# Seven block products instead of eight in two of the four feed-forward halves

## The chip, the cores and the metric

One core of a Trainium2 chip runs the whole kernel. The metric is the time of one execution in microseconds (us) on the device; three runs of the kernel before are given. A profiled execution of its own gives the trace. Engines are named as in the profile: PE is TensorE (matrix products), DVE is VectorE, ACT is ScalarE, POOL is GpSimd, SP is SyncE, which here only issues transfers.

## The reference

Two layers run over 512 tokens of width 1024 (256 context tokens and 256 latent tokens, two streams with their own modulation vectors). Each layer is: a feed-forward half step, a token mixing, and a second feed-forward half step.

```
x = x + 0.5 * mx[2] * _swiglu(_modulate(_rmsnorm(x, g_n1[l]), mx[0], mx[1]), w_ff1_up[l], w_ff1_dn[l])
...
def _swiglu(h, w_up, w_dn):
    a, b = jnp.split(h @ w_up, 2, axis=-1)
    return (jax.nn.silu(a) * b) @ w_dn
```

`w_up` is 1024 x 5632 (gate part a and up part b of 2816 columns each), `w_dn` is 2816 x 1024, all float32. The nine modulation rows `mx[0..8]` of a layer come from `silu(c) @ w_ada[l]`. After the last layer only the latent stream is needed.

## The kernel before

Activations lie with the channels on the 128 partitions and the tokens in the columns: context tokens are columns 0 to 255 (`CTX`), latent tokens 256 to 511 (`LAT`). The hidden width 2816 is 22 blocks of 128 (`FB`). The four halves are called (layer, half): (0,0), (0,1), (1,0), (1,1); the last one handles the latent stream alone. Halves (0,1) and (1,0) follow each other directly, between the two mixings.

**Float32 by parts.** An operand is split into a float32r part (hi) and the rest (lo). A product is three matmuls: hi by hi, hi by lo, lo by hi. Activations after a norm lie in `hh` and `hl`; the gated hidden blocks lie in pairs of their own.

**Weights.** A weight comes in units of 128 x 1024 float32 (512 KB) by the SP queue into a buffer `st` (3 of them). ACT makes `wh` from it (line 224) and DVE makes `wl = st - wh` (line 226). There are `WB` = 5 pairs `wh`, `wl`. A unit is issued up to `AHEAD` = 150 places ahead of the work that uses it, where buffers allow.

**A feed-forward half** (`ff`): the 22 hidden blocks go in two chunks of 11. For each block `i`, the up product gives `pa` (gate) and `pb` (up) in PSUM, 2 x 8 x 3 matmuls of 512 columns; then tanh, three DVE operations and one ACT copy make the gated block and its two parts. After 11 blocks the down product runs: 8 output blocks of 33 matmuls, each added to the residual `x` (line 481). In the second chunk the last two output blocks go by streams, the latent stream first, so that the norm of a stream (`Norm`, `rstd_of`, `newton`, `norm_apply`) runs beside the other's products; the `flush` in the next half's first block does the context norm.

**Modulation.** `Ada` computes modulation columns on DVE: each block of 128 columns is two transfers of 256 KB by the POOL queue and two or four multiply-and-accumulate operations of 128 x 512 (line 375). The blocks are dripped into half (0,0) (56 blocks) and half (0,1) (all 72 of layer 1).

The order of the instructions on each engine is fixed when the program is built, by a scheduler that follows program order and the places ahead; an engine runs its row strictly in that order. Two queues of transfers matter, SP's and POOL's.

Of the kernel before, what the change touches and what calls it, by code (L numbers as in the profile page):

```python
# [8 lines left out]
F32 = mybir.dt.float32  # L9
# [7 lines left out]
P = 128  # L17
# [25 lines left out]
WB = 5  # L43
# [37 lines left out]
def _unit_index():  # L81
    idx, n = {}, 0
    for l in range(DEPTH):
        for ff in range(2):
            if ff == 1:
# [18 lines left out]
                for nb in range(KB):  # L104
                    idx[("out", l, nb)] = n
                    n += 1
            for c in range(2):
# [16 lines left out]
def body(ctx, tc, A):  # L124
# [6 lines left out]
    ap_ = ctx.enter_context(tc.tile_pool(name="ap", bufs=56))  # L131
# [22 lines left out]
    def put_aside():  # L154
        """The residual leaves its room to the token mixing, which needs it only at its end."""
        for j in range(KB):
            nc.sync.dma_start(aside[:, j, :], xs[j])
# [53 lines left out]
    def load(dst, src):  # L211
        """On the SP queue, and at the start behind what the first norm needs."""
# [3 lines left out]
    def unit(key, n, kb):  # L216
        with tc.high_priority(offset=ahead[0]):
            st = wp.tile([P, UW], F32, tag="st", name="st")
# [11 lines left out]
    def units(keys, n, kb):  # L230
        """A weight cut along its rows: a list of (hi, lo) [P, N] blocks."""
# [7 lines left out]
    def mm3(ps, lhs, rhs, lsl=slice(None), rsl=slice(None), late=False):  # L239
        """late: the second parts of rhs come last, as they are not there yet."""  # L240
# [39 lines left out]
    # The engine holds one set of functions at a time: Tanh is in one, Ln in another,  # L280
    # Exp in both.
# [12 lines left out]
    def tanh_half(out, src):  # L294
        """2 sigmoid(x) - 1"""
# [3 lines left out]
    def silu2(out, src):  # L299
        """2 x sigmoid(x)"""  # L300
# [10 lines left out]
    def silu_rows():  # L311
        """Twice the silu of the two conditioning vectors on every partition, in halves."""
# [79 lines left out]
    class Ada:  # L392
        """Modulation blocks, fed into other work; loads run some blocks ahead."""
# [10 lines left out]
        def run(self, frac):  # L404
            """Until this share of the blocks is done."""
# [15 lines left out]
    def newton(r, ss, n, width, t=None):  # L421
        """One step that takes r = rsqrt(ss / width + EPS) to float32's accuracy."""
# [5 lines left out]
    def rstd_of(sq_sum, n, width):  # L428
        """sq_sum: to be summed over the partitions, and over its list."""
# [10 lines left out]
    class Norm:  # L440
        """Sum of squares over the blocks of one stream, added as they come."""
# [26 lines left out]

    def hpairs(cols):
# [4 lines left out]
    def flush():  # L474
        """The norm that a stream still lacks."""
# [99 lines left out]
    def mix(l, after):  # L575
# [12 lines left out]
        class Feed:  # L588
            """Work that stands between the steps of the attentions, whose steps wait
            for each other: products that need no other result soon (step), and the  # L590
            elementwise chains behind them, an operation at a time (pump)."""
# [28 lines left out]
            def advance(self, i):  # L620
                """One step of this item; whether it had one left."""
# [12 lines left out]
            def step(self, n=1, open_=lambda key: True):  # L634
                """n steps of the first items that there is room for."""
# [19 lines left out]
        # two blocks of the queries' width: a bank each, or one for both  # L655
# [13 lines left out]
        def split_gen(jobs, scale=None):  # L669
            """jobs: (source, hi, lo)."""  # L670
# [10 lines left out]
        def conv_start(ps):  # L681
            """The tokens of two segments, each between zeros."""
# [100 lines left out]
            # minus the stabiliser, exactly, and its parts for the product that spreads it  # L783
# [17 lines left out]
        def gate_cols():  # L801
            """As columns of tokens."""
# [17 lines left out]
        def log_sigm(f, e):  # L820
            """f becomes log sigmoid(f)."""
# [9 lines left out]
        # latent projections of the attention  # L831
# [22 lines left out]
        def rope_gen(z, c0, then):  # L854
            """In place on the latent columns of z, which start at c0; then the parts."""
# [13 lines left out]
        def head_parts(z, dst):  # L869
            """By head: both parts of the queries one over the other, as the rows of one product."""  # L870
# [565 lines left out]
```

## Time and profile before

| | |
|---|---|
| three runs | 2394.9, 2396.31, 2396.78 us (median 2396.31) |
| profiled execution, from its first to its last instruction | 2395.4 us |
| PE busy | 98% of the span |
| DVE, ACT, POOL busy | 67%, 41%, 7% |
| half (0,1) | 1030 to 1402 us: first chunk to 1159, its down product to 1220, second chunk to 1343, its down product to 1402 |
| half (1,0) | 1402 to 1775 us: first chunk to 1534, its down product to 1595 |
| mixings | 410 to 1030 us and 1775 to 2190 us |

The span is the profiled execution's whole time, and the medians of the runs are of other executions of the same program; they differ by 0.9 us. A stretch's limit is read from the stretch: an engine that is busy 67% over the whole may be full in one part of it.

### The profile page before, as it was taken

Reading aid. Unit: us, or ns where it says so; the run is one execution under the profiler, and the core shown is the slowest. Engines: PE = TensorE matmul, PEld = TensorE weight load, DVE = VectorE, ACT = ScalarE, POOL = GpSimd, SP = SyncE. Lnnn points to the kernel's source line nnn. Section 1 sums busy time; section 2 is a strip of 40 time slices with the busy share of each in tenths; the row PEclk is TensorE's granted clock in tenths of the full one; section 3 lists DMA queues with packets and bytes.
Section 4 is the critical chain, followed back from the end, with each engine's and each line's share of the span. In section 5 each row is a group of like instructions: output and inputs, shape, how many; then the busy total and the mean of one; then the engine's idle time right before and its main releaser. Section 6 shows DMA issues by size and latency. Waiting matters only on the chain.

```text
span 2395.4 us, 34542 instructions
## 1 busy us (share of the span) xinstructions
PE 2352.9 (98%) x13170; PEld 2008.8 (84%) x13170; DVE 1601.3 (67%) x3375; ACT 990.7 (41%) x1630; POOL 171.9 (7%) x384
## 2 busy tenths in 40 slices
PE   8999999999999999999999999999999999999998
PEld 4888888888888888888888898888887799999998
DVE  7887777786477654479986663334357867776665
ACT  6322223556555442242222242222245654555443
POOL 1112110000010000012231000000000000000000
PEclk9999999999999999999999999999999999999999
DMA  8656444211122222355585322232232223354563
GB/s 317 204 168 228 150 146 158 86 56 53 62 80 71 72 79 97 132 194 186 202 299 187 115 101 99 78 116 89 76 103 80 99 80 106 103 170 152 175 209 117
DMA packets 101251, 316.93 MB, mean 132 GB/s; under 512 B 13150, under 2 KB 15454, under 8 KB 101086
## 3 DMA queue, kind: packets, MB, share of 16 engines
q1 hardware_dynamic: 80606, 247.61, 30.3%
q0 software_dynamic: 20480, 67.13, 8.1%
q8 instruction: 103, 1.69, 0.3%
q14 instruction: 62, 0.51, 0.1%
HBM read 311.54 MB, written 3.15 MB: 131 GB/s over the span
## 4 chain that ended last, share of the span: by engine, by line
PE 95%; DVE 3%; ACT 2%; issue 1%; DMA 0%; DVEq 0%; SPq 0%; ACTq 0%
PE dn L246 20%; PE pa L270 5%; PE pb L270 5%; PE pb L272 5%; PE pa L272 5%; PE pa L271 5%; PE pb L271 5%; PE p L270 4%; PE p L271 4%; PE p L272 4%; PE sc L1159 2%; PE pv L246 2%; PE pa L246 2%; PE pb L246 2%; PE k L270 1%; PE k L271 1%
## 5 line engine op out<-in xcount | busy, mean ns | idle before, releaser
L224 ACT ACTIVATE wh<-st 128x1024 fp32r<-128x1024 f32 (+1 forms) x484 | 471.3, 976 | 945.3 <-PE pb L271 253.6
L226 DVE TENSOR_TENSOR wl<-st,wh 128x1024 fp32r<-128x1024 f32 (+1 forms) x484 | 540.4, 1119 | 374.2 <-ACT wh L224 370.3
L246 PE MATMUL dn<-hi,wl 128*128 128x512 f32 (+1 forms) x674 | 247.7, 367 | 0.0
L246 PE MATMUL dn<-hi,wh 128*128 128x512 f32 (+1 forms) x674 | 247.3, 368 | 0.0
L246 PE MATMUL dn<-lo,wh 128*128 128x512 f32 (+1 forms) x674 | 246.5, 366 | 0.0
L270 PE MATMUL pa<-hh,wh 128*128 128x512 f32 (+1 forms) x640 | 234.4, 366 | 0.0
L270 PE MATMUL pb<-hh,wh 128*128 128x512 f32 (+1 forms) x640 | 234.4, 366 | 0.0
L272 PE MATMUL pa<-hh,wl 128*128 128x512 f32 (+1 forms) x640 | 234.2, 366 | 0.0
L272 PE MATMUL pb<-hh,wl 128*128 128x512 f32 (+1 forms) x640 | 234.2, 366 | 0.0
L271 PE MATMUL pa<-hl,wh 128*128 128x512 f32 (+1 forms) x640 | 234.2, 366 | 0.0
L271 PE MATMUL pb<-hl,wh 128*128 128x512 f32 (+1 forms) x640 | 234.2, 366 | 0.0
L364 POOL DMA_DIRECT2D ada<-ada x256 | 137.2, 537 | 736.0 <-PE dn L246 216.1
L271 PE MATMUL p<-hl,wh 128*128 128x256 f32 (+1 forms) x536 | 179.6, 335 | 0.0
L270 PE MATMUL p<-hh,wh 128*128 128x512 f32 (+1 forms) x512 | 174.1, 340 | 0.0
L272 PE MATMUL p<-hh,wl 128*128 128x512 f32 (+1 forms) x512 | 172.6, 337 | 0.0
L375 DVE SCALAR_TENSOR_TENSOR ada<-ada,cs 128x512 f32<-128x512 f32 x256 | 166.3, 684 | 0.0
L246 PEld LDWEIGHTS dn<-hi,wh 128*128 128x128 f32 x674 | 126.7, 188 | 23.4
L246 PEld LDWEIGHTS dn<-hi,wl 128*128 128x128 f32 x674 | 126.6, 188 | 22.7
L246 PEld LDWEIGHTS dn<-lo,wh 128*128 128x128 f32 x674 | 126.7, 188 | 22.4
L270 PEld LDWEIGHTS pb<-hh,wh 128*128 128x128 f32 x640 | 120.2, 188 | 22.0
L272 PEld LDWEIGHTS pb<-hh,wl 128*128 128x128 f32 x640 | 120.0, 188 | 22.1
L272 PEld LDWEIGHTS pa<-hh,wl 128*128 128x128 f32 x640 | 120.0, 188 | 22.1
(361 smaller groups left out, 4979.1 us busy)
## 6 DMA issues: line engine op xcount, KB each, us to landing
st<-wall SPq DMA_DIRECT2D x340, 512.0 KB, 3.3
ada<-ada POOLq DMA_DIRECT2D x256, 256.0 KB, 3.4
st<-wall SPq DMA_DIRECT2D x72, 384.0 KB, 2.9
st<-wall SPq DMA_DIRECT2D x64, 320.0 KB, 2.9
ada<-ada SPq DMA_DIRECT2D x32, 256.0 KB, 5.4
x<-xT SPq DMA_DIRECT2D x8, 256.0 KB, 5.8
cb<-cc SPq DMA_DIRECT2D x8, 256.0 KB, 5.8
aside<-x SPq DMA_DIRECT2D x8, 256.0 KB, 2.0
```

The costliest lines, as they stand in the source:

```text
L224: S.activation(hi[:, :n], st[:, :n], AF.Copy)
L226: V.tensor_tensor(lo[:, :n], st[:, :n], hi[:, :n].bitcast(F32), ALU.subtract)
L246: TE.matmul(ps, lhs[k][a][:, lsl], rhs[k][b][:, rsl], start=i == 0, stop=i == 3 * n - 1)
L270: TE.matmul(ps, a, b, start=first, stop=False)
L271: TE.matmul(ps, a, bl, start=False, stop=False)
L272: TE.matmul(ps, al, b, start=False, stop=final_)
L364: nc.gpsimd.dma_start(st, ada[ADA[l, g] + j, :, q * 512 : (q + 1) * 512])
L375: V.scalar_tensor_tensor(o, st, 0.5, cb[s, q], ALU.mult, ALU.mult, accum_out=dst)
L1159: TE.matmul(ps[qb], a[:, c], b[:, :nk], start=i == 0, stop=i == len(steps) - 1)
```

## The change

In halves (0,1) and (1,0) the up product of two hidden blocks (a "step"; 11 steps) is written as a product of 2 x 2 blocks. The weight's blocks are a11, a12, a21, a22: the first digit is the part (1 gate, 2 up), the second the half of the 1024 rows. The activation's blocks are the latent and context tokens of each half of the rows. Eight block products become seven: products 1, 2, 3 and 4 have one factor that is a plain block, and 5, 6, 7 work on sums (weights a21+a22, that plus a11, a11+a21; a12 is added for product 3). A block product is 24 matmuls of 256 columns (2 blocks, 4 row blocks, 3 parts). The results are combined where PSUM is read.

- Sums of weights: a21+a22 and the sum with a11 by GpSimd, in place in `st` (L591 of the changed kernel); a11+a21 and the sum with a12 by accumulating transfers of the POOL queue (L589).
- Sums of activations: `seven_lat` and `seven_ctx` take the place of `norm_apply` before these halves; they make the activation sums and their two parts.
- Each of the seven weights of a step is split into two parts (before: four units for the same two blocks).
- Three chunks of 8, 8 and 6 hidden blocks, so three down products (24, 24 and 18 matmuls for each output block) instead of two of 33. Steps run two at a time, interleaved product by product.
- Buffers: `WB` 5 to 4, `st` 3 to 6, activation tiles 56 to 54.
- `Ada`: 24 blocks of layer 1 in half (0,1), the other 48 in half (1,0); before, 72 and none.

```diff
-WB = 5
+AHEAD_S = 110
+SEVEN = ((0, 1), (1, 0))
+STEPS = FB // 2
+STEP_GROUPS = (((0, 1), (2, 3)), ((4, 5), (6, 7)), ((8, 9), (10,)))
+WB = 4
+STB = 6
...
-    ap_ = ctx.enter_context(tc.tile_pool(name="ap", bufs=56))
+    ap_ = ctx.enter_context(tc.tile_pool(name="ap", bufs=54))
...
+        h = {}
+        for a in range(2):
+            for q in range(2):
+                h[a, q] = t = act(F32, "h7")[:, :T].rearrange("p (k t) -> p k t", k=2)
+                for i in range(2):
+                    j = 4 * a + 2 * q + i
+                    V.scalar_tensor_tensor(t[:, i], xs[j][:, nm.cols], mod(l, s, g + 1, j), r, ALU.mult, ALU.mult)
+                    S.activation(t[:, i], t[:, i], AF.Identity, bias=mod(l, s, g, j))
+        return h
+
+    def split7(t, hi, lo):
+        S.activation(hi, t, AF.Copy)
+        V.tensor_tensor(lo, t, hi.bitcast(F32), ALU.subtract)
...
+        ORDER = (1, 2, 5, 6, 7, 4, 3)
+        BANK = {1: 0, 6: 0, 7: 0, 4: 0, 2: 1, 5: 2, 3: 2}
+        NEW = {1: ("a", "a11"), 2: ("b", "a12"), 5: ("c", "a21")}
+        ADD = {5: "d", 6: "a"}
+        MORE = {7: ("a", "a21"), 3: ("c", "a12")}
...
+        def weights(self, r):
+            with tc.high_priority(offset=AHEAD_S):
+                if r in self.NEW:
+                    self.load(*self.NEW[r])
+                if r == 5:
+                    self.load("d", "a22")
+                if r in self.MORE:
+                    n, q = self.MORE[r]
+                    nc.gpsimd.dma_start(self.st[n], self.src(q), accum_op=ALU.add)
+                if r in self.ADD:
+                    G.tensor_tensor(self.st["c"], self.st["c"], self.st[self.ADD[r]], ALU.add)
+                st = self.st[{1: "a", 2: "b", 5: "c", 6: "c", 7: "a", 4: "d", 3: "c"}[r]]
+                hi, lo = wsplit(st, UW)
+            w = "p (b k n) -> p b k n"
+            return hi.rearrange(w, b=2, k=4), lo.rearrange(w, b=2, k=4)
...
+            for k in range(4):
+                bh, bl = hx[r][k]
+                for p in range(2):
+                    o = ps[:, p * HALF : (p + 1) * HALF]
+                    for i, (w, x) in enumerate(((hi, bh), (hi, bl), (lo, bh))):
+                        TE.matmul(
+                            o, w[:, p, k], x, start=r in (1, 2, 5) and k + p + i == 0,
+                            stop=k == 3 and p == 1 and i == 2, skip_group_check=True,
+                        )
...
+            V.scalar_tensor_tensor(t, t, -0.5, b, ALU.mult, ALU.mult)
+            for i in range(2):
+                hi, lo = self.dst[i]
+                src = t[:, i * HALF : (i + 1) * HALF]
+                S.activation(hi[:, cols], src, AF.Copy)
+                V.tensor_tensor(lo[:, cols], src, hi[:, cols].bitcast(F32), ALU.subtract)
+
+        def after(self, r):
+            v, ps = self.v, self.ps
+            if r in (1, 6, 7):
+                v[r] = self.tile("s7")
+                S.activation(v[r], ps[0], AF.Copy)
+            if r == 2:
+                a = self.tile("a7")
+                V.tensor_tensor(a, ps[1], v[1], ALU.add)
+                v["lat"] = self.gated(a)
+            elif r == 7:
+                v["b"] = self.tile("b7")
+                V.tensor_tensor(v["b"], ps[2], v[7], ALU.add)
+            elif r == 4:
+                self.out(v["lat"], ps[0], LAT)
+            elif r == 3:
+                a = self.tile("a7")
+                V.tensor_tensor(a, ps[2], v[6], ALU.add)
+                self.out(self.gated(a), v["b"], CTX)
...
+                for r in Step.ORDER:
+                    for s in steps:
+                        s.product(r)
+                        if r == 1:
+                            flush()
+                        s.after(r)
+                        drip(1 / 7)
...
-        ff(l, 0, [0, 1], Ada(0, range(2, 9), 2) if l == 0 else None, lambda nm, s, l=l: norm_apply(nm, l, s, 3))
...
-            ff(l, 1, [0, 1], Ada(l + 1, range(9), 2), lambda nm, s, l=l: norm_apply(nm, l + 1, s, 0))
...
+        half(0, Ada(0, range(2, 9), 2) if l == 0 else Ada(l, range(3, 9), 2), apply(None, l, 3))
+        mix(l, apply(1, l, 6))
+        half(1, None if last else Ada(l + 1, range(3), 2), final if last else apply(0, l + 1, 0))
```

The first place is DVE's row in half (0,1), some 100 operations after the first operation of the latent norm. `wl` is the low part of a weight, `ada`, `junk`, `mod` and `mhalf` belong to the modulation blocks, `lo` is the low part of a hidden block, `r2` and `s7` are a product in PSUM and its saved partner, `a7` and `t7` the gate. After the change, up to the weight of product 5 of the second pair's second step:

```order
L390 SCALAR_TENSOR_TENSOR ada_9965,mod11_112<-ada_9965,cs_9729 128x512
L390 SCALAR_TENSOR_TENSOR ada_9967,mhalf_108<-ada_9967,cs_9734 128x512
L638 TENSOR_TENSOR a7_10335<-r2_10310,s7_10259 128x512
L629 TENSOR_TENSOR lo_9603<-t7_10212,hi_9602 128x256
L629 TENSOR_TENSOR lo_9605<-t7_10212,hi_9604 128x256
L638 TENSOR_TENSOR a7_10371<-r2_10346,s7_10292 128x512
L317 SCALAR_TENSOR_TENSOR t7_10337<-t7_10337,a7_10335 128x512
L390 SCALAR_TENSOR_TENSOR junk_10444,mod10_111<-ada_10105,cs_9719 128x512
L390 SCALAR_TENSOR_TENSOR junk_10447,mhalf_108<-ada_10107,cs_9724 128x512
L317 SCALAR_TENSOR_TENSOR t7_10373<-t7_10373,a7_10371 128x512
L390 SCALAR_TENSOR_TENSOR ada_10105,mod11_112<-ada_10105,cs_9729 128x512
L556 TENSOR_TENSOR wl_10416<-st_10410,wh_10415 128x1024
```

Before, in the same half, where `sg` is the gate and `pa`, `pb` the products in PSUM:

```order
L302 SCALAR_TENSOR_TENSOR sg_10054<-sg_10054,pa_9992 128x512
L375 SCALAR_TENSOR_TENSOR ada_9960,mhalf_108<-ada_9956,cs_9931 128x512
L226 TENSOR_TENSOR wl_10363<-st_10360,wh_10362 128x1024
L375 SCALAR_TENSOR_TENSOR ada_9968,mod11_112<-ada_9968,cs_9926 128x512
L375 SCALAR_TENSOR_TENSOR ada_9970,mhalf_108<-ada_9970,cs_9931 128x512
L538 SCALAR_TENSOR_TENSOR sg_10054<-sg_10054,pb_9993 128x512
L226 TENSOR_TENSOR wl_10393<-st_10390,wh_10392 128x1024
L541 TENSOR_TENSOR lo_9607<-sg_10054,hi_9606 128x512
```

A weight's low part stood between single operations before; now eleven others stand between two of them here. From the first operation of the latent norm in half (0,1) to the last row of the first piece, DVE has 17 weight splits of 128 x 1024, 63 operations of 128 x 512 (19 of them of `Ada`) and 28 of 128 x 256. In half (1,0) the like stretch, to the weight of product 6 of the second pair's second step, has 18, 80 (36 of `Ada`) and 28.

The second place is POOL's row at the start of half (0,1), where `st` are the weight buffers. After the change:

```order
L591 TENSOR_TENSOR st_9860<-st_9860,st_9862 128x1024
L591 TENSOR_TENSOR st_9894<-st_9894,st_9896 128x1024
L591 TENSOR_TENSOR st_9860<-st_9860,st_9606 128x1024
L589 DMA st_9606<-wall 128x1024
L591 TENSOR_TENSOR st_9894<-st_9894,st_9745 128x1024
L589 DMA st_9745<-wall 128x1024
L589 DMA st_9860<-wall 128x1024
L589 DMA st_9894<-wall 128x1024
L379 DMA ada_9737<-ada 128x512
```

Before, the same queue held nothing but the modulation's transfers there:

```order
L364 DMA ada_9934<-ada 128x512
L364 DMA ada_9936<-ada 128x512
L364 DMA ada_9938<-ada 128x512
L364 DMA ada_9940<-ada 128x512
L364 DMA ada_9948<-ada 128x512
```

Additions of whole weight blocks now stand ahead of the transfers, and an accumulating transfer waits in the queue for the split of the buffer that it changes.

## Rows read from the trace of the kernel before

**Rows 1.** The page: span, busy time of the engines, chain that ended last.

```profile
span 2395.4 us, 34542 instructions
PE 2352.9 (98%) x13170; PEld 2008.8 (84%) x13170; DVE 1601.3 (67%) x3375; ACT 990.7 (41%) x1630; POOL 171.9 (7%) x384
PE 95%; DVE 3%; ACT 2%; issue 1%; DMA 0%; DVEq 0%; SPq 0%; ACTq 0%
```

**Rows 2.** Windows of both halves and the first mixing; columns in the first row.

```profile
core 0: us, PE busy (x) PEld busy (x) DVE busy (x) ACT busy (x) POOL busy (x), PEclk, DMA share, GB/s
1030.00:1159.00 129.00, 126.84 (x634) 106.37 (x633) 112.90 (x278) 44.89 (x71) 28.38 (x54) 0.99 0.59 200
1159.00:1220.00 61.00, 61.00 (x265) 49.24 (x264) 59.60 (x168) 15.11 (x19) 18.86 (x36) 1.00 0.65 224
1402.00:1534.00 132.00, 130.96 (x664) 110.02 (x663) 64.84 (x103) 46.27 (x73) 0.00 (x0) 0.99 0.26 92
410.00:1030.00 620.00, 617.41 (x3361) 521.58 (x3361) 394.02 (x836) 297.68 (x555) 23.12 (x72) 1.00 0.23 80
```

**Rows 3.** The chain in order of time: start, duration, work and count.

```profile
1052.62 2.80 PE pa L246 x24
1159.02 61.35 PE dn L246 x264
2260.39 31.31 PE dn L246 x264
```

**Rows 4.** The same chain around the start of half (1,0).

```profile
1402.06 3.94 PE dn L246 x33
...
1406.03 1.06 ACT wh L224
```

**Rows 5.** DVE's timeline in half (0,1): start, busy, line, operation, shape, count.

```profile
1058.89 2.36 DVE L226 TENSOR_TENSOR wl<-st,wh 128x1024 fp32r<-128x1024 f32 x2 [0.21 <-ACT wh L224]
1061.17 0.69 DVE L302 SCALAR_TENSOR_TENSOR cs<-cs,cb 128x512 f32<-128x512 f32 x1
...
1170.62 0.69 DVE L375 SCALAR_TENSOR_TENSOR junk<-ada,cs 128x512 f32<-128x512 f32 x1
...
1171.23 0.69 DVE L375 SCALAR_TENSOR_TENSOR junk<-ada,cs 128x512 f32<-128x512 f32 x1
...
1187.42 0.47 DVE L481 SCALAR_TENSOR_TENSOR x<-dn,mod,x 128x256 f32<-128x256 f32 x1
1187.82 0.68 DVE L375 SCALAR_TENSOR_TENSOR junk<-ada,cs 128x512 f32<-128x512 f32 x1
```

**Rows 6.** POOL's timeline in the mixings: masks of 128 columns.

```profile
643.43 0.29 POOL L974 TENSOR_SCALAR_AFFINE_SELECT e<-e 128x128 f32<-128x128 f32 x1 [134.45 <-PE s L246]
...
664.28 4.41 POOL L974 TENSOR_SCALAR_AFFINE_SELECT e<-e 128x128 f32<-128x128 f32 x4 [18.70 <-ACT e L970]
...
721.82 2.63 POOL L974 TENSOR_SCALAR_AFFINE_SELECT e<-e 128x128 f32<-128x128 f32 x4 [9.01 <-ACT e L970]
...
1975.74 1.76 POOL L974 TENSOR_SCALAR_AFFINE_SELECT e<-e 128x128 f32<-128x128 f32 x3 [48.41 <-ACT e L970]
```

**Rows 7.** DVE's timeline beside such masks.

```profile
664.18 1.28 DVE L712 SCALAR_TENSOR_TENSOR sg<-sg,cv 128x512 f32<-128x512 f32 x2
665.38 1.22 DVE L226 TENSOR_TENSOR wl<-st,wh 128x1024 fp32r<-128x1024 f32 x1
666.51 1.29 DVE L678 SCALAR_TENSOR_TENSOR kl<-sg,kh 128x512 fp32r<-128x512 f32 x2
...
723.45 0.85 DVE L705 SCALAR_TENSOR_TENSOR cv<-cpd,vecs,cv 128x512 f32<-128x512 f32 x1
...
1975.79 1.31 DVE L226 TENSOR_TENSOR wl<-st,wh 128x1024 fp32r<-128x1024 f32 x1
```

**Rows 8.** The page's list of transfers: count, size of one, median us to landing.

```profile
st<-wall SPq DMA_DIRECT2D x340, 512.0 KB, 3.3
ada<-ada POOLq DMA_DIRECT2D x256, 256.0 KB, 3.4
```

More of the change, by code (lines that the diff above doesn't have):

```diff
@@ L106, in _unit_index @@
                     n += 1
+            if (l, ff) in SEVEN:
+                for t in range(STEPS):
+                    for q in ("a11", "a12", "a21", "a22"):
+                        idx[("up7", l, ff, t, q)] = n
+                        n += 1
+                for c in range(len(STEP_GROUPS)):
+                    for nb in range(KB):
+                        idx[("dn7", l, ff, c, nb)] = n
+                        n += 1
+                continue
             for c in range(2):
@@ L217, in unit @@
         with tc.high_priority(offset=ahead[0]):
-            st = wp.tile([P, UW], F32, tag="st", name="st")
+            st = wp.tile([P, UW], F32, tag="st", name="st", bufs=STB)
             load(st[:, :n], wall[UNITS[key], :, :n])
@@ new lines, in split7, with seven_ctx, room, keep @@
+    def split7(t, hi, lo):
+        S.activation(hi, t, AF.Copy)
+        V.tensor_tensor(lo, t, hi.bitcast(F32), ALU.subtract)
+    def seven_ctx(nm, l, g):
+        r = nm.rstd()
+        L, C = hx.pop("lat"), shifted(nm, l, 0, g, r)
+        def room(name, q):
+            t = act(F32, name)[:, :T]
+            return t, t.rearrange("p (k t) -> p k t", k=2)
+        def keep(key, q, t, hi=None, lo=None):
+            if hi is None:
+                hi, lo = (act(F32R, n)[:, :T].rearrange("p (k t) -> p k t", k=2) for n in ("dh", "dl"))
+            split7(t, hi, lo)
+            hx.setdefault(key, []).extend((hi[:, k], lo[:, k]) for k in range(2))
+        d5, d6 = {}, {}
+        for key in (5, 6, 7, 4, 3):
+            hx.pop(key, None)
+        for q in range(2):
+            _, d5[q] = room("d5", q)
+            V.tensor_tensor(d5[q], L[0, q], C[0, q], ALU.subtract)
+            keep(5, q, d5[q], hh[:, 2 * q : 2 * q + 2, CTX], hl[:, 2 * q : 2 * q + 2, CTX])
+        for q in range(2):
+            _, d6[q] = room("d6", q)
+            V.scalar_tensor_tensor(d6[q], d5[q], -1.0, C[1, q], ALU.mult, ALU.subtract)
+            keep(6, q, d6[q])
+        for q in range(2):
+            _, d = room("d7", q)
+            V.tensor_tensor(d, C[1, q], C[0, q], ALU.subtract)
+            keep(7, q, d)
+        for q in range(2):
+            _, d = room("d4", q)
+            V.scalar_tensor_tensor(d, d6[q], -1.0, L[1, q], ALU.mult, ALU.subtract)
+            keep(4, q, d)
+        for q in range(2):
+            keep(3, q, C[1, q], hh[:, 4 + 2 * q : 6 + 2 * q, CTX], hl[:, 4 + 2 * q : 6 + 2 * q, CTX])
@@ new lines, in ff7, with drip, make @@
+    def ff7(l, f, queue, after):
+        g0 = 0 if f == 0 else 6
+        done = [0.0]
+        total = STEPS + len(STEP_GROUPS) * KB * 2 / 7 - 3
+        def drip(w):
+            done[0] += w
+            if queue:
+                queue.run(min(1.0, done[0] / total))
+        for c, groups in enumerate(STEP_GROUPS):
+            gs = []
+            for group in groups:
+                steps = []
+                for t in group:
+                    dst = [pair(T) for _ in range(2)]
+                    gs += dst
+                    steps.append(Step(l, f, t, dst))
+                for r in Step.ORDER:
[5 more added lines that the diff above has]
+                        drip(1 / 7)
+            def make(nb, c=c, nk=len(gs)):
+                r = units([("dn7", l, f, c, nb)], nk * P, nk)
+                drip(2 / 7)
+                return r
+            norms = {s: Norm((CTX, LAT)[s]) for s in (0, 1)} if c + 1 == len(STEP_GROUPS) else None
+            last_blocks(make, gs, [0, 1], l, g0 + 2, norms, lambda s: after(norms[s], s))
+        if queue:
+            queue.run(1.0)
@@ L1323, in body, with apply, half @@
         last = l == DEPTH - 1
-        ff(l, 0, [0, 1], Ada(0, range(2, 9), 2) if l == 0 else None, lambda nm, s, l=l: norm_apply(nm, l, s, 3))
-        mix(l, lambda nm, s, l=l: norm_apply(nm, l, s, 6))
-        if last:
-            ff(l, 1, [1], None, final)
-        else:
-            ff(l, 1, [0, 1], Ada(l + 1, range(9), 2), lambda nm, s, l=l: norm_apply(nm, l + 1, s, 0))
+        def apply(f, l_, g):
+            do = seven if (l_, f) in SEVEN else norm_apply
+            return lambda nm, s: do(nm, l_, s, g)
+        def half(f, queue, after):
+            if (l, f) in SEVEN:
+                ff7(l, f, queue, after)
+            else:
+                ff(l, f, [1] if last and f else [0, 1], queue, after)
+        half(0, Ada(0, range(2, 9), 2) if l == 0 else Ada(l, range(3, 9), 2), apply(None, l, 3))
+        mix(l, apply(1, l, 6))
+        half(1, None if last else Ada(l + 1, range(3), 2), final if last else apply(0, l + 1, 0))
 def _pack(I):
@@ L1368, in _pack @@
             u = I[up][l].reshape(D, 2, FB, P)
+            if (l, ff) in SEVEN:
+                u7 = I[up][l].reshape(2, 4, P, 2, STEPS, 2, P)
+                for t in range(STEPS):
+                    for m in range(2):
+                        for k in range(2):
+                            unit(("up7", l, ff, t, f"a{m + 1}{k + 1}"), np.ascontiguousarray(u7[k, :, :, m, t].transpose(1, 2, 0, 3)))
+                d = I[dn][l].reshape(FB, P, KB, P)
+                i0 = 0
+                for c, groups in enumerate(STEP_GROUPS):
+                    i1 = i0 + 2 * sum(len(g) for g in groups)
+                    for nb in range(KB):
+                        unit(("dn7", l, ff, c, nb), np.ascontiguousarray(d[i0:i1, :, nb].transpose(1, 0, 2)))
+                    i0 = i1
+                continue
             for i in range(FB):
```

39 lines of the change are left out of this document (added).

## The prediction

> **What bounds the kernel now.** I read the page first, then windows by stage, then the chain, then single engines. The page says that PE is busy 98% of the span and carries 95% of the chain that ended last [rows 1]. So only two things can shorten the kernel: fewer columns through PE, or less of the little time that PE waits. The windows say the same for the two halves that are changed: PE is full, but for 2.2 us at the start of half (0,1) (129.00 less 126.84) and 1.0 us at the start of (1,0) [rows 2]. The second thing that the reader is to see there is DVE. Over the kernel it is at 67%, in the first chunk of (0,1) at 112.90 of 129 us and in the down product behind it at 59.60 of 61: this stretch has no room on DVE. In the first chunk of (1,0) it is at 64.84 of 132, since no modulation blocks run there.
>
> **What PE saves.** A step (two hidden blocks) is 96 matmuls of 512 columns before. The chain gives 61.35 us for 264 such matmuls, 0.2324 each, and 2.80 us for 24 of 256 columns, 0.1167 each [rows 3]. So 96 x 0.2324 = 22.31 becomes 168 x 0.1167 = 19.61: 2.70 a step, and **-59.5 us** for 22 steps. The first two blocks ran in halves of 256 columns already, at the same cost. The down products keep their 66 matmuls for each output block. The added ACT copies out of PSUM, and the three splits more of each step, cost nothing on ACT where it stays ahead of DVE: it was busy 44.89 of 129 us in the first chunk of (0,1) [rows 2], a split takes it 1.06 [rows 4], and three more for each of four steps are 13 us. Without that cover each would be 1.06 of wait.
>
> **What DVE has to do, and where it is late.** DVE's pitch, from start to start, is 1.14 us for a weight split (two from 1058.89 to 1061.17), 0.61 for an operation of 512 columns, 0.40 for one of 256 [rows 5]. A step of the new form has seven splits (8.0), seven operations of 512 (4.3) and four of 256 (1.6): 13.9 us, beside 19.6 on PE. That fits, also with 1.6 modulation blocks a step in (0,1), four operations each (3.9). But the first chunk starts with the norms, with the activation sums and their parts, and with the modulation's first blocks, all in DVE's one row. Up to the weight of product 5 of the second pair's second step, the order has 17 splits, 63 operations of 512 and 28 of 256: 17 x 1.14 + 63 x 0.61 + 28 x 0.40 = 69.0 us from the first operation of the latent norm. PE needs that weight after 19 products, 53.2 us. It is 15.8 us late. In (1,0), to the weight of product 6 of the second pair's second step, there are 18, 80 and 28: 80.9 (with 0.3 for small ones) against 21 products, 58.8: 22.1 late. Behind these places the splits of the next weights follow each other with little between them (1.14 against 2.80), so DVE catches up and PE is late once in each half. PE waited 2.2 and 1.0 us at these starts before, which goes: 15.8 + 22.1 - 3.2 = **+34.7 us**. This is where most of the gain is given back.
>
> **What covers a norm.** At the end of (0,1) 33 matmuls, 3.94 us, stood behind the latent norm's sum [rows 4]; with a last chunk of six blocks it is 18, 2.1 us. What is late next is the first product of the following stage: 1.8 us at the start of (1,0) and at the start of the second mixing, **+3.6 us**.
>
> **What GpSimd's additions cost.** No addition of GpSimd of this size is in the trace, so I bound it. GpSimd and DVE hold each other up: a mask of 128 columns takes 0.29 us alone, but four take 4.41 from 664.28 [rows 6], where DVE runs without a gap from 664.18 to 667.80 [rows 7]. The other way, a split that meets a mask takes 1.31 instead of 1.22, and an operation of 512 columns that meets one from the group at 721.82 takes 0.85 instead of 0.69 [rows 5 to 7]. So a mask takes 0.09 to 0.16 us from DVE, and eight times its columns 0.7 to 1.3. Below is nothing, if an addition falls in a gap; above is the whole of eight masks, 2.3. I take 1.0 (what was seen to be taken from DVE, not what GpSimd itself needs). Six additions lie in each of the two late stretches, where each counts in full: **+12 us**, with 0 and +28 as the ends. Elsewhere DVE has the room: 13.9 + 3.9 + 2 x 1.0 is 19.8 a step, against 19.6 and the four weights that are ready at a chunk's start.
>
> By the Trainium skill (page "SBUF — State Buffer", section "Who interferes with whom") a VectorE instruction with two inputs in SBUF contends with a GpSimd instruction that reads SBUF, and whoever issues first keeps the shared port for the whole instruction. That agrees with the 4.41 us above; it speaks for the upper end, 8 x 0.29, and the sum would then be 16 us higher. The skill's "GPSIMD Engine Reference" (section 3.1) gives 4497 ns for an addition of twice these columns, so as an estimate 2.2 us here, and by it the sum would be 14 us higher.
>
> **What the transfers cost.** The same bytes move: up weights in four blocks a step, before in four units. A transfer by SP lands in 3.3 us, one of POOL's, half as large, in 3.4 [rows 8]. An accumulating one is not in the trace. Product 7's weight needs GpSimd's addition for product 6, then the transfer, the ACT split (1.06) and the DVE split (1.14), 5.6 us with a landing of 3.4. If product 6 is itself just in time, PE needs it 1.06 + 1.14 + 2 x 2.80 = 7.8 us after the same addition. So up to 5.6 us of landing it costs nothing; the lower bound is that, the upper a landing of three times as long, 10.2, with 4.6 us for each of 12 groups of steps. I take nothing in the sum, since both landings that are seen lie below 5.6. In POOL's queue the modulation's transfers stand behind these, and they run two blocks ahead.
>
> **The mixings** have one pair of weight parts and two activation tiles less. PE idles only 2.6 us of 620 in the first [rows 2], so the pool as it is covers nearly all. With 4 pairs of 5 I allow 0 to 10 us, and take **+3**, about as much again as it waits now.
>
> **The sum.** -59.5 + 34.7 + 3.6 + 12 + 3 = -6.2 us. The profiled span is 2395.4, so 2389.2; the median of the runs shown lies 0.9 above that span, so **2390 us**. I call less than 0.2% (4.8 us) no change, which is about what a measurement of this kernel can tell.
>
> **Rivals.**
>
> *DVE is not late, and the additions fall into gaps.* The late terms assume that DVE goes through its row without the order mattering, and that PE starts full at the norm's end. If the additions cost nothing (-12) and some of the modulation's operations or norm parts overlap what PE still has to do (say a fifth of 34.7), the time is 2371. For it: elsewhere DVE has much room, 64.84 of 132 us in (1,0) [rows 2]. Against it: an engine keeps its row's order, and the counts are the order's. 2362 to 2381.
>
> *GpSimd's addition holds DVE for all its time (slower).* At 2.3 us instead of 1.0 it is 12 x 1.3 = 16 us more, 2406. If, besides, it finds no gap and starts only when DVE stands at the very split that it feeds, ACT's 1.06 comes on the path too: 13 more, 2418. For it: the four masks in 4.41 us, which waited out a row of DVE's operations [rows 6, 7]. Against it: the 0.09 and 0.16 that DVE itself lost. It decides from a price of 1.9 us: (2401 - 2390) / 12 = 0.9 above mine.
>
> *The accumulating transfer lands late.* It reads and writes its target. At twice the 3.4 it is 6.8, 1.2 us beyond the cover, for 12 groups 14 us, 2405; at three times 55 us, 2445. For it: nothing in the trace shows such a transfer. Against it: most have more than one product of lead, since weights are issued up to 110 places ahead.
>
> *Matmuls of 256 columns do not run at half the time.* 264 of them in the last down product took 31.31 us [rows 3], 0.1186 each instead of 0.1167. At that rate the 22 steps save 52.5, and the time is 2397: no change. For it: PE then takes turns between weights more often. Against it: the 24 of the same kind of product as here ran at 0.1167.
>
> **How the numbers follow.** My forecast (2383 to 2399, its own range) 0.33, of which 0.18 lies under the bound for faster and 0.15 within it. DVE not late 0.26, all faster. The addition holds DVE 0.22, all slower. The late transfer 0.09, slower. The slow matmul 0.10: 0.02 faster, 0.06 same, 0.02 slower. Faster 0.46, same 0.21, slower 0.33. The range goes from 2364, near the lower end of the first rival, to 2418, the far end of the second, and leaves out some 0.1 of the late transfer and 0.07 at the lower end.
>
> **What would show it.** In the changed profile PE should have about 168 x 0.1167 us in each step, and its idle time should lie in the first chunk of (0,1) and of (1,0), some 20 and 25 us, ended by the low part of a weight (DVE). DVE should be without gaps in those stretches. GpSimd's additions should show durations of 1 to 2.3 us, with DVE operations drawn out beside them. I am wrong if PE's waits lie evenly over all chunks (a rate, not a start: additions or transfers), if the waits end on a transfer, or if the mixings grow by more than 10 us.

## The result, and the profile after

The changed kernel takes 2511.76 us (median of 4 runs, 2508.35 to 2516.27); the kernel before took 2396.55 beside it. The ratio is 1.048, with a 95% interval from 1.047 to 1.050: 115 us slower, where 2390 was forecast and 2418 was the end of the range.

The page of the changed kernel, whose lines answer to [rows 1] and [rows 8]:

```profile
span 2506.6 us, 37771 instructions
PE 2336.1 (93%) x14502; PEld 2065.6 (82%) x14502; DVE 1808.0 (72%) x3571; ACT 1108.4 (44%) x1814; POOL 337.5 (13%) x472
...
PE 76%; DVE 9%; DMA 5%; issue 4%; ACT 3%; POOL 2%; SPq 0%; ACTq 0%; POOLq 0%; DVEq 0%
...
st<-wall SPq DMA_DIRECT2D x372, 512.0 KB, 3.6
...
st<-wall POOLq DMA_DIRECT2D x44, 512.0 KB, 6.9
```

PE carried 95% of the chain that ended last and carries 76% now. The rest went to DVE, transfers, ACT, POOL and issue. PE's busy time hardly fell (2352.9 to 2336.1) although it has 59.5 us less to do, which the next view explains. Windows of the first and second chunk of half (0,1) and of the first chunk of (1,0), to be held against [rows 2]:

```profile
core 0: us, PE busy (x) PEld busy (x) DVE busy (x) ACT busy (x) POOL busy (x), PEclk, DMA share, GB/s
1028.00:1166.00 138.00, 95.01 (x677) 92.56 (x676) 103.19 (x157) 61.50 (x97) 39.73 (x31) 0.80 0.49 135
1213.00:1306.00 93.00, 83.10 (x672) 81.06 (x671) 80.22 (x115) 42.10 (x58) 32.26 (x27) 0.98 0.61 173
1460.00:1595.00 135.00, 94.66 (x699) 92.13 (x698) 115.80 (x211) 63.72 (x101) 46.52 (x43) 0.84 0.53 160
```

Each of these chunks has 672 matmuls of 256 columns, 78.4 us at 0.1167. The first takes 138 us, the second 93, the first of (1,0) 135. The third window has 27 other matmuls in it, most of them of the half before; from its own first product, at 1468, that chunk takes 127. PE waits in all of them, and the granted clock falls with the waits: 0.80 in the first chunk, a mean between the two levels of 1.2 and 2.4 GHz, where PE is busy 95 us with the work of 78.4 and five other matmuls.

What PE waited for (total, times, longest):

```profile
PE r L608 <- ACT s L635: 71.0, 14, 18.5
PE r L608 <- ACT wh L555: 19.5, 10, 6.3
PE r L608 <- DVE wl L556: 13.4, 11, 3.0
...
PE r L608 <- ACT hh L509: 9.5, 2, 5.6
```

The largest row is none that the prediction names: the copy (L635) by which ACT saves the PSUM bank of product 1, so that product 6 can be added in it. The longest of these waits in the first chunk of (0,1) ends at 1072.07, after 17.8 us. The chain of the changed kernel shows what lies behind it:

```profile
1045.71 7.53 POOL st L591
...
1055.46 2.69 POOL st L591
...
1059.74 5.52 DMA st<-wall
...
1065.36 1.07 ACT wh L555
...
1067.70 0.33 SPq L579
...
1069.16 10.90 DMA cb<-cc
...
1082.19 0.49 ACT s L635
```

Two additions of GpSimd, one of 7.53 us, then an accumulating transfer, then a split. The transfer `cb<-cc` behind them brings the conditioning vector for the modulation; it stands in SP's queue behind weights that found no free buffer. ACT's own row in the same stretch:

```profile
1053.28 1.06 ACT L555 ACTIVATE wh<-st 128x1024 fp32r<-128x1024 f32 x1 [4.92 <-POOL st L591]
...
1065.36 1.06 ACT L555 ACTIVATE wh<-st 128x1024 fp32r<-128x1024 f32 x1 [3.10 <-DMA st<-wall]
...
1068.91 0.63 ACT L509 ACTIVATE dh<-d 128x512 fp32r<-128x512 f32 x1 [1.98 <-DVE d L544]
1070.90 0.63 ACT L509 ACTIVATE dh<-d 128x512 fp32r<-128x512 f32 x1 [1.36 <-DVE d L544]
1071.44 0.58 ACT L635 ACTIVATE s<-r 128x512 f32<-128x512 f32 x1
```

ACT runs its row in order. The copy at 1071.44 needs only product 1, long done, but stands behind the splits for products 6 and 7, and those wait for the sums of weights. Behind the last of them it stands 5 us more behind parts of the activation sums (L509), which wait for DVE.

### The profile page after: what moved, and what is told of

It reads as the page before. It is cut to its first block, busy times and chain, and to the rows that moved or that the text cites. A ratio compares the mean times of both kernels' runs of the same rounds, so it can differ in the third digit from the quotient of the medians.

```text
span 2506.6 us, 37771 instructions
## 1 busy us (share of the span) xinstructions
PE 2336.1 (93%) x14502; PEld 2065.6 (82%) x14502; DVE 1808.0 (72%) x3571; ACT 1108.4 (44%) x1814; POOL 337.5 (13%) x472
## 4 chain that ended last, share of the span: by engine, by line
PE 76%; DVE 9%; DMA 5%; issue 4%; ACT 3%; POOL 2%; SPq 0%; ACTq 0%; POOLq 0%; DVEq 0%
PE dn L261 19%; PE r L608 6%; DMA st<-wall 4%; PE p L285 4%; PE p L286 4%; PE p L287 4%; PE sc L1376 2%; PE pb L286 2%; PE pa L286 2%; PE pb L285 2%; PE pa L285 2%; PE pb L287 2%; PE pa L287 2%; PE pv L261 2%; DVE wl L556 2%
## 5 line engine op out<-in xcount | busy, mean ns | idle before, releaser
L241 DVE TENSOR_TENSOR wl<-st,wh 128x1024 fp32r<-128x1024 f32 (+1 forms) x380 | 430.2, 1136 | 215.4 <-ACT wh L239 212.2
L555 ACT ACTIVATE wh<-st 128x1024 fp32r<-128x1024 f32 x154 | 159.7, 1054 | 257.9 <-PE dn L261 85.0
L556 DVE TENSOR_TENSOR wl<-st,wh 128x1024 fp32r<-128x1024 f32 x154 | 194.6, 1281 | 72.7 <-ACT wh L555 72.6
L608 PE MATMUL r<-dh,wh 128*128 128x256 f32 x528 | 160.0, 303 | 80.9 <-ACT s L635 71.0
L608 PE MATMUL r<-hh,wh 128*128 128x256 f32 x704 | 202.4, 288 | 19.0 <-ACT wh L555 9.5
L591 POOL TENSOR_TENSOR st<-st 128x1024 f32<-128x1024 f32 x44 | 127.0, 2892 | 587.7 <-DVE wl L556 278.3
L608 PE MATMUL r<-hh,wl 128*128 128x256 f32 x704 | 201.3, 287 | 4.7 <-DVE wl L556 4.7
L608 PE MATMUL r<-hl,wh 128*128 128x256 f32 x704 | 200.6, 286 | 0.0
L608 PE MATMUL r<-dh,wl 128*128 128x256 f32 x528 | 157.2, 298 | 8.8 <-DVE wl L556 8.7
L608 PE MATMUL r<-dl,wh 128*128 128x256 f32 x528 | 156.5, 296 | 0.0
```

What stands on the lines that cost most here:

```text
L241: V.tensor_tensor(lo[:, :n], st[:, :n], hi[:, :n].bitcast(F32), ALU.subtract)
L555: S.activation(hi[:, :n], st[:, :n], AF.Copy)
L556: V.tensor_tensor(lo[:, :n], st[:, :n], hi[:, :n].bitcast(F32), ALU.subtract)
L591: G.tensor_tensor(self.st["c"], self.st["c"], self.st[self.ADD[r]], ALU.add)
L608: TE.matmul(o, w[:, p, k], x, start=r in (1, 2, 5) and k + p + i == 0, stop=k == 3 and p == 1 and i == 2, skip_group_check=True,)
```

## The experiments

Four questions: does the place of the copy in ACT's row cost the time (A), do GpSimd's additions (B), do the accumulating transfers (C), or VectorE's first chunks as forecast? All times are medians; the kernel before took 2396.1 to 2397.5 beside them.

**The copy ahead of the splits.**

```diff
-        S.activation(hi[:, :n], st[:, :n], AF.Copy)
+        with tc.issue_after(behind_) if behind_ else nullcontext():
+            S.activation(hi[:, :n], st[:, :n], AF.Copy)
...
-                hi, lo = wsplit(st, UW)
+                hi, lo = wsplit(st, UW, self.copied if r in (6, 7) else None)
```

(`self.copied` is the step's latest copy out of PSUM: after product 1 for the split of product 6, after product 6 for that of product 7.) 

> Computes the whole reference. Theory A (ScalarE's row: the copy that frees a PSUM bank after product 1 stands behind the splits of products 6 and 7, so whatever makes those splits late stops PE): PE's waits for the copy, 71 us in the changed kernel, mostly go, and the time falls by 30 to 50 us, to 2462 to 2482. Rival B (the sums of weights are late by themselves): the waits only move to the splits of products 6 and 7, and the time falls by under 15 us.

Measured: 2494.19 us, 18 less than the changed kernel. That lies between the two expectations, nearer to B's. What PE waits for has moved, not gone:

```profile
PE r L609 <- ACT wh L556: 61.6, 24, 11.7
PE r L609 <- DVE wl L557: 24.9, 23, 2.8
```

The waits for copies have become waits for the splits behind the sums. The copy was where the lateness showed, not its cause.

**Without GpSimd's additions.**

```diff
-                    G.tensor_tensor(self.st["c"], self.st["c"], self.st[self.ADD[r]], ALU.add)
+                    pass
```

> Leaves out GpSimd's additions (a21+a22 and the sum with a11), so products 5 and 6 use plain blocks. Theory B (GpSimd's additions are late: they took 2.9 us on average, one 7.5, and hold VectorE): the time falls by 40 to 70 us, to 2442 to 2472. Rival C (the accumulating transfers set the pace): under 15 us.

Measured: 2419.56 us, 92 less; more than B's upper end. Now the second chunk runs at PE's pace, 79.10 us. The window of its products (tile `r`), and the page's row of engines for this kernel:

```profile
1187.90:1267.00 79.10, 78.96 (x672) 78.95 (x672) 9.58 (x14) 6.94 (x12) 1.00 0.66 185
...
PE 2318.9 (96%) x14502; PEld 2052.8 (85%) x14502; DVE 1740.8 (72%) x3571; ACT 1109.1 (46%) x1814; POOL 211.3 (9%) x428
```

DVE issues the same 3571 instructions and is busy 1740.8 us instead of 1808.0. So 44 additions drew its operations out by 67 us, 1.5 each.

**Plain transfers for the accumulating ones.**

```diff
-                    nc.gpsimd.dma_start(self.st[n], self.src(q), accum_op=ALU.add)
+                    nc.gpsimd.dma_start(self.st[n], self.src(q))
```

> The accumulating transfers become plain ones into the same buffers from the same queue, so products 7 and 3 use a21 and a12 alone. Theory C (an accumulating transfer lands in 6.9 us instead of 3.6, and the splits behind it wait): the time falls by 20 to 40 us, to 2472 to 2492. Rival B: under 10 us, since GpSimd's additions ahead of it in the same queue are what is late.

Measured: 2475.8 us, 36 less, within C's expectation. Both kinds of sum cost, each with the other in place.

**Without any sum.** Both edits, with the plain loads on SP's queue. 

> Leaves out both kinds of sums: no additions of GpSimd, and plain loads by SP's queue instead of accumulating transfers. If the sums (B, C), however ScalarE's row is ordered, are the loss, 80 us go and the time is about 2430, which leaves the 35 us of VectorE's first chunks; if it is the order of ScalarE's row alone or VectorE's work, it stays over 2470.

Measured: 2404.08 us, 108 less than the changed kernel, and still 6.6 above the kernel before beside it (2397.52). Beyond the expectation (2430) in the direction of B and C: with the additions gone the transfers are worth 15.5 more, with both in place 36, so the two overlap (92 + 36 is more than 108). Windows of this kernel that count only the seven products' instructions (tile `r`; columns as above without POOL), in the first and second chunk of (0,1) and the first of (1,0):

```profile
1034.00:1133.40 99.40, 85.98 (x672) 84.96 (x672) 9.60 (x14) 6.86 (x12) 0.90 0.53 168
1180.40:1259.40 79.00, 78.87 (x672) 78.93 (x672) 9.59 (x14) 6.96 (x12) 1.00 0.57 179
1407.80:1513.00 105.20, 87.45 (x672) 86.31 (x672) 9.54 (x14) 6.78 (x12) 0.89 0.57 180
```

The second chunk shows the new form undisturbed: 79.0 us for four steps. The first chunks are 20.4 and 26.2 us longer, with no sum of weights in the kernel; 15.7 of these 46.6 us are PE busy for longer with the same matmuls, with a granted clock of 0.90 and 0.89, means between the same two levels. PE's row and ACT's show where the longest wait of the first chunk of (0,1) stands:

```profile
1063.18 0.58 PE L608 MATMUL r<-dh,wh 128*128 128x256 f32 x1 [6.68 <-ACT s L635]
...
1060.02 0.63 ACT L509 ACTIVATE dh<-d 128x512 fp32r<-128x512 f32 x1 [1.98 <-DVE d L544]
1062.01 0.63 ACT L509 ACTIVATE dh<-d 128x512 fp32r<-128x512 f32 x1 [1.36 <-DVE d L544]
1062.55 0.58 ACT L635 ACTIVATE s<-r 128x512 f32<-128x512 f32 x1
```

1063.18 is the start of the seventh product of the chunk, and all six waits for such copies (25.0 us in both halves) stand at the seventh, eighth and ninth. The copy again stands behind parts of the activation sums, and these wait for DVE.

**The additions on VectorE.**

```diff
-                    G.tensor_tensor(self.st["c"], self.st["c"], self.st[self.ADD[r]], ALU.add)
+                    V.tensor_tensor(self.st["c"], self.st["c"], self.st[self.ADD[r]], ALU.add)
```

> The whole reference; the same additions on VectorE instead of GpSimd. Theory B (an addition on GpSimd, 2.9 us, waits for a gap in VectorE's row and holds VectorE while it runs): 1.14 us on VectorE is cheaper than that, and the time falls by 40 to 65 us, to 2447 to 2472. Rival (VectorE has no room for 44 more operations, 50 us): it falls by under 15 us or rises.

 Measured: 2462.01 us, 50 less, as B has it. Against the kernel without GpSimd's additions they cost 42 us here, for 47 us of VectorE's row (busy 1787.5 us by the page, 1740.8 without).

**Both edits: additions on VectorE and the copy ahead.** 

> The whole reference; additions on VectorE, and the copy after product 1 ahead of the splits of products 6 and 7 on ScalarE. Theory A adds 10 to 20 us to what the additions on VectorE alone gain: 2430 to 2455. If the order of ScalarE's row matters only where the sums are late, under 6 us more than with the additions on VectorE alone.

 Measured: 2448.17 us, 14 less than the additions on VectorE alone, the amount that A expects. It is the fastest kernel with all 22 steps in the new form that still computes the sums, and 52 above the kernel before.

**No sums, and the copy ahead.** 

> Leaves out both kinds of sums (plain loads by SP's queue), with the copy ahead of the splits. Without sums PE still waited 25 us for those copies. Theory A: these go and the time is 2375 to 2390, below 2396. Rival (VectorE's row at the start of the halves is what is late, the copies only stand behind it): 2398 to 2408, with the waits moved to the splits.

 Measured: 2415.25 us, 11 more than without that order. This is a miss for both: it lies outside A's range, and above the rival's, although the waits did move to the splits, as the rival has it (24 us in 10 waits). The order of ACT's row helps where sums are late (18 and 14 us) and costs where they are not, so A is no cause of its own.

**No sums, and the modulation of layer 1 in half (0,0).**

```diff
             self.todo = [(l, g, j) for g in groups for j in range(8)]
+            if l == 0:
+                self.todo += [(1, g, j) for g in range(9) for j in range(8)]
```

> Leaves out both kinds of sums, and computes all of layer 1's modulation in half (0,0), which gets longer; so only the stretches of halves (0,1) and (1,0) are compared, not the whole time. If VectorE's modulation work and its late loads are what is late in the first chunks, these shrink from 99 and 105 us to 80 to 88; if the order of ScalarE's row is, they stay over 95.

 The whole time, 2457.72 us in one run, has the longer half (0,0) in it. Measured in windows of tile `r`, the first chunks:

```profile
1116.90:1211.80 94.90, 83.64 (x672) 83.06 (x672) 10.18 (x15) 6.86 (x12) 0.91 0.42 125
...
1480.40:1573.80 93.40, 82.79 (x672) 82.18 (x672) 10.17 (x15) 6.85 (x12) 0.93 0.40 121
```

They shrink by 4.5 and 11.8 us, to 94.9 and 93.4; neither expectation is met in full. Of the 47 us that the first chunks lose without sums, the modulation's work is 16. The other 30 stay; the waits for copies that are left (8.7 and 8.6 us) stand at the seventh product, behind the activation sums. No run takes the norms and the activation sums away alone.

**Additions that nobody waits for.**

```diff
-                    G.tensor_tensor(self.st["c"], self.st["c"], self.st[self.ADD[r]], ALU.add)
+                    side = act(F32, "side")
+                    for i in range(2):
+                        x = slice(i * 512, (i + 1) * 512)
+                        G.tensor_tensor(side[:, :512], self.st["c"][:, x], self.st[self.ADD[r]][:, x], ALU.add)
```

> As the kernel without sums (2404), but GpSimd does additions of the same sizes and at the same places (two of 512 columns for one of 1024) into a tile that nothing reads. If an addition costs by holding VectorE up, the time rises by 40 to 80 us, to 2444 to 2484. If what costs is that the next split waits for its result, it rises by under 15 us, to below 2420.

Measured: 2482.55 us, 78 more than without sums, as the first reading has it. No split waits for these results, and DVE's busy time is up by 85 us (1739.7 to 1824.4 by the pages):

```profile
PE 2335.0 (94%) x14502; PEld 2065.1 (83%) x14502; DVE 1824.4 (74%) x3571; ACT 1108.3 (45%) x1814; POOL 311.3 (13%) x472
```

DVE's row and POOL's in the second chunk of (0,1) show the hold itself:

```profile
1204.68 6.92 DVE L390 SCALAR_TENSOR_TENSOR ada<-ada,cs 128x512 f32<-128x512 f32 x1
...
1204.72 8.05 POOL L594 TENSOR_TENSOR side<-st 128x512 f32<-128x512 f32 x6
```

One operation of DVE took 6.92 us, beside six additions that followed each other without a gap. So additions cost this much by holding DVE up, with nobody waiting for their results. It is not an exact split of the 92 us. Two operations stand here for one, and they hold DVE 85 us instead of 67. Their reads also hold buffers back from their next load; but ACT's splits waited only 11.3 us, in 5 waits, for a transfer. In the changed kernel ACT waited 41.3 us, in 15 waits, for the sums themselves, and how much of the 92 us this lateness is, no run shows.

**The first blocks in the old form.** Three kernels keep the old form (and the old norm) for the first 6 or 8 hidden blocks of the two halves, make the activation sums on VectorE beside them, and run 8 or 7 steps in the new form behind; additions on VectorE, the copy ahead.

```diff
+PL = 6
+STEP_GROUPS = (((3, 4), (5, 6)), ((7, 8), (9, 10)))
...
+        for i in range(2, PL):
+            up(slice(0, T), hpairs(slice(0, T)), keys[i], None, gs[i])
+            for _ in range(-(-8 // (PL - 2))):
+                next(sums)
```

> The whole reference: in both halves the first 6 hidden blocks stay in the old form, with the old norm, and the activation sums are made on VectorE from the parts beside them; 8 steps in the new form behind, additions on VectorE, the copy ahead of the splits, modulation mostly in the down products. If the loss that is left is the start of the halves, PE saves 16 x 2.70 = 43 us and loses 10 to 25: 2363 to 2386. If the sums are late wherever they stand: 2400 or more.

 Measured: 2400.94 us, ratio 1.001 (1.000 to 1.002). 

> The same with 8 blocks in the old form and 7 steps in the new one, chunks of 8, 8 and 6. PE saves 14 x 2.70 = 38 us; more room for the activation sums: 2365 to 2386 by the first reading, 2400 or more by the second.

 Measured: 2410.73 us. Both miss the first reading's range and come out at the second's. The windows of the kernel with 6 blocks show why, in the first and last new chunk of (1,0):

```profile
1508.00:1614.00 106.00, 86.17 (x671) 84.35 (x670) 91.94 (x184) 43.02 (x59) 21.70 (x36) 0.89 0.66 195
...
1658.00:1738.00 80.00, 80.00 (x677) 79.77 (x676) 62.42 (x83) 42.67 (x60) 16.81 (x26) 1.00 0.73 206
```

The last one runs at full pace with its sums in it; the first loses 26 us beside a glut of modulation operations on DVE. So the second reading's words (late wherever they stand) are not borne out, though its time is.

**The same with the modulation spread by stage.**

```diff
+FR = {(0, 1): (0.125, 0.3, 0.48, 0.8, 0.92, 1.0), (1, 0): (0.125, 0.22, 0.3, 0.63, 0.78, 1.0)}
...
+                queue.run(min(1.0, lo + (fr[i] - lo) * min(1.0, at[1])))
```

> The whole reference; as the kernel with 6 blocks first in the old form (2401), with the modulation blocks spread by stage so that the one glut on VectorE (the chunk behind the first down product of half (1,0), 106 us instead of 79) goes. If VectorE's row is what is left, that chunk falls to 80 to 90 us and the time to 2370 to 2385, below the kernel before. If the new form's sums are late whatever else VectorE does, 2395 or more.

 Measured: 2398.11 us, ratio 1.0005 (0.9995 to 1.0014): no difference from the kernel before, again a miss of the time, although the chunk with the glut fell to 88 us, within the first reading. The waits became short, as the longest of the largest row shows:

```profile
PE r L616 <- DVE wl L564: 11.8, 14, 2.2
```

The glut was part of what was left, not all: 16 steps save 43 us on PE, and the rest of the kernel takes them back. Windows of this kernel, the four new chunks and, in each half, the down product between them, show where:

```profile
1137.10:1223.90 86.80, 82.49 (x673) 81.10 (x673) 72.53 (x116) 42.93 (x59) 10.56 (x15) 0.98 0.63 172
1223.90:1275.50 51.60, 48.43 (x196) 37.85 (x195) 41.01 (x103) 10.12 (x13) 8.35 (x16) 0.93 0.48 159
1275.50:1356.10 80.60, 79.82 (x672) 79.34 (x672) 66.25 (x95) 42.44 (x58) 10.38 (x14) 1.00 0.65 179
...
1509.90:1598.30 88.40, 82.13 (x673) 79.50 (x672) 76.66 (x128) 43.01 (x59) 10.53 (x15) 1.00 0.61 169
1598.30:1645.20 46.90, 45.55 (x196) 36.15 (x195) 45.91 (x124) 10.17 (x14) 18.05 (x34) 1.00 0.75 265
1645.20:1728.90 83.70, 79.45 (x673) 78.84 (x672) 67.19 (x98) 42.56 (x59) 20.19 (x32) 1.00 0.74 216
```

The new chunks lose 23.5 us against 79.0 each, and these two down products 9.3 against 44.6 (192 x 0.2324). No version here beats the kernel before.

## Why the prediction was wrong

**PE's saving (-59.5): right.** Four undisturbed steps took 79.0 us, 19.75 each, where 19.61 was worked out. That settles the fourth rival too: 78.87 us busy for 672 matmuls is 0.117 each, not 0.1186.

**VectorE late in the first chunks (+34.7): the cause in part, not the place, and too small.** Without sums of weights the first chunks still lose 46.6 us against the undisturbed chunk, where 37.9 (15.8 + 22.1) were forecast. But no wait stands at the places that the order's counts gave, the weights needed after 19 and 21 products. The waits stand after six, seven and eight products and end on ACT's copies. DVE's row is late there with the activation sums; counting it alone left out ACT, through which these sums, the weights' high parts and the copies pass in turn. That the size came near is partly luck: the sum counts DVE's 69.0 us from the norm and PE's 53.2 from the first product, as if both began at once, where in (0,1) without sums DVE began to scale the latent stream at 1030.81 and PE's first product at 1034.25. The 3.2 us taken off did not go: they were waits for the first activations, which are 9.5 now.

**GpSimd's additions (+12): the step that failed.** It failed in two ways. The price was 1.0 us, from masks that took 0.09 to 0.16 from DVE; the additions took 1.5 (67 us by 44). That is half of their 2.9 us on average; one of them blocked DVE for nearly all its time, as DVE's timeline shows, in an operation that takes 0.68 elsewhere:

```profile
1045.55 0.68 DVE L536 SCALAR_TENSOR_TENSOR d<-d,h 128x512 f32<-128x512 f32 x1
...
1050.30 0.68 DVE L536 SCALAR_TENSOR_TENSOR d<-d,h 128x512 f32<-128x512 f32 x1
1054.37 1.23 DVE L556 TENSOR_TENSOR wl<-st,wh 128x1024 fp32r<-128x1024 f32 x1 [3.39 <-ACT wh L555]
1055.52 3.19 DVE L510 TENSOR_TENSOR dl<-d,dh 128x512 fp32r<-128x512 f32 x1
```

Beside the last one POOL's addition runs from 1055.46 for 2.69 us. The other way round, the addition that began at 1045.71 lasted 7.54: DVE ran eight operations without a gap from 1045.55 to 1050.98 (the first two rows above are the first and the last of them), and from there to its end are 2.27 us, about what the shortest addition took in all (2.35). That is what the four masks in [rows 6, 7] had shown. The row was read, and put to a rival with 0.22. By the Trainium skill ("SBUF — State Buffer", "Who interferes with whom") the engine that issues first keeps the port for the whole instruction: the 3.19 agrees with it. The 7.54, a wait through several of DVE's instructions, is more than that rule says. The Trainium skill's figure for twice the columns ("GPSIMD Engine Reference", section 3.1) halves to an estimate of 2.2 us; the additions took 2.9 on average here, waiting included, by the groups of the changed kernel (count, busy us, mean ns, idle before):

```profile
L591 POOL TENSOR_TENSOR st<-st 128x1024 f32<-128x1024 f32 x44 | 127.0, 2892 | 587.7 <-DVE wl L556 278.3 <-DMA st<-wall 272.1 <-DVE ada L390 23.9
```

And only 12 of the 44 were counted, since elsewhere DVE was to have room: 19.8 us a step beside 19.6. With 1.5 an addition that sum is 20.8, over PE's time in every step, and the second chunks of both halves did take 93 and 94 us instead of 79. DVE's fullness alone would make 83 of such a chunk, and DVE was busy 80.22 of the 93 us; the rest are waits of one row for another. Taking the additions out gave 92 us back.

**The accumulating transfers (0): failed.** The bound was a landing of 5.6 us; they landed in 6.9, and in the kernel without additions in 5.6; plain ones from the same queue, with the additions kept, in 4.3. They cost 36 us, or 15.5 where no addition stands in their queue. The rival of the late transfer had the mechanism and, at twice the landing, 14 us.

**ACT's copies (nothing): wrong as stated.** Room on ACT did not cover them, since a row in order makes a copy wait for whatever split stands ahead. But the order alone is worth 18 us at most, and without late sums it costs 11 to change it.

**The norm's cover (+3.6): too small.** PE waits 3.9 and 5.6 us for the first activations of the two halves, before 2.2 and 1.0, and 3.9 at the second mixing, before 0.9: 9.3 more in all. **The mixings (+3): nothing beyond that wait.** The first one takes 620.4 us without sums and 620.6 before; from the last matmul of (1,0) to the end of the kernel are 617.6 us (from 1784.8) and 614.7 (from 1780.7), 2.9 more.

The sum by the runs: -59.5 on PE, +107.7 for the sums of weights (2511.76 less 2404.08), and 67 for what is left (2404.08 less 2396.55, plus 59.5). Of what is left 46.6 are the first chunks and 9.3 the waits for first activations. Some 14 more are the down products behind the first two chunks of each half, which without sums take 46.9, 47.7, 53.1 and 44.9 us where 192 x 0.2324 is 44.6:

```profile
1133.50:1180.40 46.90, 45.52 (x194) 35.85 (x193) 30.66 (x69) 10.75 (x14) 6.42 (x12) 1.00 0.52 170
...
1259.40:1307.10 47.70, 45.85 (x196) 36.13 (x195) 30.68 (x67) 10.84 (x14) 6.41 (x12) 1.00 0.51 170
...
1513.00:1566.10 53.10, 47.34 (x191) 36.46 (x190) 42.37 (x107) 11.17 (x15) 13.86 (x26) 0.94 0.67 220
...
1645.00:1689.90 44.90, 44.90 (x196) 36.34 (x196) 32.67 (x74) 10.47 (x14) 11.39 (x22) 1.00 0.70 237
```

Read stretch by stretch like this they make 70, 3 more than the 67. Why these down products are slower stays open, and so does why the new chunks of the last kernel keep 80.6 to 88.4 us.

## What to carry to other kernels

An engine that is off the path by its busy time can still stop the path by what it shares: here 127 us of GpSimd work drew VectorE's row out by 67 and the kernel by 92, and the same additions on VectorE were cheaper (50 us back). Where a trace shows one engine waiting out another, take the whole instruction as the price (2.1 us of the kernel's time for an addition here), and count it in every step, not only where the row is already full. An algebraic saving on the engine that is the bound must be held against every operation that it adds on the engines that feed it, in the order in which they run.

## What the runs showed of the hardware that was not expected

- PE's waits cost twice: in the first chunk of (0,1) the granted clock was 0.80, and the matmuls that take 79 us in a full chunk kept PE busy for 93.6 (the windows of tile `r`).
- An accumulating transfer of 512 KB landed in 6.9 us (median); a plain one from the same queue, in its place, in 4.3, and one from SP's queue in 3.6.
- VectorE and GpSimd hold each other for whole instructions, and for several in a row: 3.19 us for an operation of 0.68, 6.92 for one beside six additions of 512 columns, and 7.54 for an addition whose shortest neighbours took 2.4.
